# Letting the shared expert's products run until the first block's down products, and loading ScalarE's silu table ahead of that block

## The chip, the cores and the metric

One core of a Trainium2 chip runs one layer of a decoder in one launch. The metric is the device time of one execution in microseconds (us). The engines are named as in the profile: PE (TensorE matmul), PEld (its weight loads), DVE (VectorE), ACT (ScalarE), POOL (GpSimd), SP (SyncE, which issues the weight transfers).

## What is computed

The reference is one layer on 256 tokens of width 1024: a mixer (convolution, differential attention, gates), then a mixture of experts. The change touches the second half alone:

```python
def moe_ffn(h, ...):                       # t: 256 tokens x 1024
    scores = sigmoid(t @ w_router)         # 64 experts, group-limited top 8
    gates = ...                            # weight of each token for each expert, 0 for most
    g, u = split(t_e @ w_gu[e])            # each expert: 1024 -> 2 x 256
    routed += (silu(g) * u * gate) @ w_down[e]      # 256 -> 1024
    sg, su = split(t @ w_sh_gu)            # the shared expert, for all tokens
    shared = (silu(sg) * su) @ w_sh_down
    return routed + shared
```

Weights and activations are float32. The 64 experts' weights are 3 MB each (2 MB gate/up, 1 MB down), 192 MB in all, and each is read once.

## The kernel before

The kernel is written as some forty Python generators (fibers), one for each strand of work. A planner (class `Plan`, lines 49 to 184) runs them against its own costs and due times: each `yield` names an engine and a cost, an event or a buffer; whichever fiber can start first, or has the higher priority in `PRIO` among those that start nearly together, issues its instruction next. The order in which instructions are issued is the order in each engine's queue, which the engine then works through from the front. So a line that changes when an event is set can move instructions on every engine. On the chip, an instruction waits on semaphores for what it reads and for the buffer that it writes, not for the planner's events.

Once the router has chosen, the experts are grouped into 28 **blocks** of 128 token slots, by kind: P (two experts of 64 slots), H (one of 128), M, and Q (four of 32). Blocks 0, 1 and 2 are of kind P, block 3 of kind Q. `experts` (L1793 on) goes through the blocks in order, all on PE's queue. For a block it issues

- the gate/up products of all its experts (L1802, one pass over k = 0 to 7),
- the combine of the block before (L1710, which scatters the down products back to tokens), then the transposes of the block's activations (L1823), which wait for ACT's silu (L1672) and DVE's scaling (L1676),
- the gather of a later block's tokens (L1523) and that block's slot tables (L1564, L1567; a copy on ACT, L1584),
- the down products (L1849), which wait for ACT's copy of the transposes (L1685).

Weights are loaded by SP (L270) in one fixed list, in order, into 1 MB slots. A load waits in SP's queue until PE has read the last of what its slot held: after k = 3 or 7 of a gate/up pass, or after a block's down products, whose `done` frees their slots (here named late_w for blocks 0 and 2).

The **shared expert** is a fiber of priority 0, `shared` (L1771 on): 32 products of 128x256 (L1784; each stands as two rows in the trace), two halves of the weights by two halves of the tokens (bank 76 takes tokens 0 to 127, bank 79 the rest). When a half of the tokens is done, `shared_tail` (L1637 on, through `gate_up`) does silu on ACT, a product on DVE (L1619), two transposes (L1625), a copy on ACT (L1629) and four down products of 128x512 (L1647), each pair of which DVE scales (L1650) before POOL adds it (L1653). Before the change, `shared` goes on freely until block 0's tokens are gathered (event "blk" 0), and from then on waits for "static", which is set after block 3's gate/up.

`overflow` (L1443 on) lists the tokens for which an expert had no slot: a ladder of tiny products and DVE operations (L1446 to L1479). `gathers` (L1583 on) gathers the tokens of blocks 0 and 1 and then sets their "blk" events.

Of the kernel before, what the change touches and what calls it, by code (L numbers as in the profile page):

```python
# [13 lines left out]
AF = mybir.ActivationFunctionType  # L14
# [161 lines left out]
def TS(n):  # L176
    return "D", 0.13 + 0.00052 * n
# [10 lines left out]
def AP(n, table=None):  # L188
    return "A", 0.06 + 0.00082 * n, table
# [6 lines left out]
def MM(n):  # L196
    return "P", n / 2400.0
# [3 lines left out]
def tile_hybrid_block(ctx, tc, x, c, positions, w_ada, b_ada, norm1_g, w_in, conv_dw, conv_dw_b,  # L201
# [3 lines left out]
    nc = tc.nc  # L205
# [7 lines left out]
    pl = Plan()  # L213
# [246 lines left out]
    iop = cst.tile([P, 1], F32, name="iop")  # L460
# [826 lines left out]
    warm = cst.tile([P, 1], F32, name="warm")  # L1287
# [198 lines left out]
    def evacuate(xt, f, p, p3, ns, b0):  # L1486
        for f2 in range(2):
            k = f + f2
            e = yield TS(ns) if not b0 and f % 4 == 0 else AP(ns)
            if e == "A":  # L1490
                nc.scalar.activation(xt[:, k, 0:ns], p3[:, f2, 0:ns], AF.Identity, bias=b2c[:, k:k + 1],  # L1491
                                     scale=a2c[:, k:k + 1])
            else:
                nc.vector.tensor_scalar(xt[:, k, 0:ns], p3[:, f2, 0:ns], a2c[:, k:k + 1], b2c[:, k:k + 1],
                                        op0=OP.mult, op1=OP.add)
        pl.put("bank", p)
        pl.set("xt", b0, f // 2)
# [3 lines left out]
    def compare(b0, t, r_):  # L1501
        pm_ = tables[b0]
        for i, (kd, js) in enumerate(blocks[b0:b0 + 2]):
            rows = rows_of[kd]
            n, m = len(rows), rows[0][1]
            if kd == "M":
                yield "D", 0.4
                for j, (o, m) in zip(js, rows):
                    nc.vector.tensor_scalar(pm_[:, t, i * P + o:i * P + o + m], iot256[:, 0:m], r_[:, t, j:j + 1],
                                            None, op0=OP.is_equal)  # L1510
            else:
                yield TT(P)
                o = pm_[:, t, i * P:(i + 1) * P].rearrange("p (n m) -> p n m", n=n)
                nc.vector.tensor_tensor(o, iot256[:, None, 0:m].to_broadcast([P, n, m]),
                                        r_[:, t, js[0]:js[0] + n, None].to_broadcast([P, n, m]), op=OP.is_equal)

    def moved(b0, p, f, ts):
        ns = P * len(blocks[b0:b0 + 2])
        p3 = p.rearrange("p (f s) -> p f s", f=2)
        for f2 in range(2):  # L1520
            for t in ts:
                for a in range(2):
                    nc.tensor.matmul(p3[:, f2, 0:ns], xr[:, a, t, (f + f2) * P:(f + f2 + 1) * P],  # L1523
                                     tables[b0][:, t, 0:ns], start=(f2 + t + a == 0), stop=(f2 + t + a == 3))
        return p3

    def opened(b0, xt):
        users = [len(blocks[b0:b0 + 2])]
        for i in range(users[0]):
            info = Weights()  # L1530
            info.xt, info.whole, info.users = xt[:, :, i * P:(i + 1) * P], xt, users
            pl.events["info", b0 + i] = info
# [55 lines left out]
    def gathers():  # L1588
        tables[0] = yield Get("pm")
        held = []  # L1590
        for t in range(2):
            pl.cur.prio = PRIO["gathers" if t else "compare"]
            yield pl.ev("rx", t)
            yield from compare(0, t, rxp[0])
            for q in range(2):
                yield pl.ev("xr", t, q)
            if t:
                pl.set("first_pm")
                opened(0, (yield Get("xt")))
            for f in range(0, K, 2):  # L1600
                if not t:
                    held.append((yield Get("bank")))
                yield MM(4 * 2 * P)
                p3 = moved(0, held[f // 2], f, (t,))
                if t:
                    pl.spawn(evacuate(pl.events["info", 0].whole, f, held[f // 2], p3, 2 * P, 0))
        for b in range(2):
            pl.set("blk", b)
        for b in range(2):
            yield from slots(b)  # L1610
# [157 lines left out]
    def shared():  # L1768
        w = None
        pgs = []  # L1770
        for q in range(2):  # L1771
            for t in range(2):
                for k in range(4 * q, 4 * q + 4):
                    yield pl.ev("h2", t, k)
                    if not k:
                        pgs.append((yield Get("bank")))
                    yield pl.ev("L", "sg", 0, k // 2)
                    w = loaded["sg", 0]
                    yield w.at[k]
                    if pl.ev("blk", 0).t is not None:  # L1780
                        yield pl.ev("static")
                    for c_ in (slice(0, 256), slice(256, 512)):
                        yield MM(4 * 256)
                        nc.tensor.matmul(pgs[t][:, c_], h2T[:, k, t * P:(t + 1) * P], w.k[k][:, c_],  # L1784
                                         start=(k + c_.start == 0), stop=(k == K - 1 and c_.start > 0))
                if q:
                    pl.spawn(shared_tail(t, pgs[t]))
            done(("sg", 0), q)

    def experts():  # L1790
        for b, (kd, js) in enumerate(blocks):
            yield pl.ev("blk", b)
            info = pl.events["info", b]  # L1793
            pg = yield Get("bank")
            for k in range(K):
                yield pl.ev("xt", b - b % 2, k // 2)
                for j in js:
                    yield pl.ev("L", "g", j, k // 2)
                    yield loaded["g", j].at[k]
                yield "P", 0.87  # L1800
                for e, o, m in tiles_of[kd]:
                    nc.tensor.matmul(pg[o:o + m], info.xt[:, k, o:o + m], loaded["g", js[e]].k[k],  # L1802
                                     start=(k == 0), stop=(k == K - 1))
                if b < 2 and k % 4 == 1:
                    for j in js:
                        if loaded["g", j].off[k // 4] != LAST:
                            advance(pl.cur.ready, loaded["g", j].off[k // 4])
                if k % 4 == 3:
                    for j in js:
                        done(("g", j), k // 4)  # L1810
            if b == NS // 2:
                pl.set("static")
            info.users[0] -= 1
            if not info.users[0]:
                pl.put("xt", info.whole)
            pl.spawn(activate(b, pg))
            if b:
                for h in range(2):
                    yield from combine(b - 1, h)
            yield pl.ev("act", b)  # L1820
            yield "P", 0.3
            for f in range(2):
                nc.tensor.transpose(pg[:, f * P:(f + 1) * P], info.act.rearrange("s (c f) -> s f c", f=2)[:, f], ident)  # L1823
            pl.put("act", info.act)
            pl.spawn(turned(b, pg))
            ahead = b + 2 - b % 2
            if ahead < len(blocks):
                if ahead == 2:
                    fs = (0, 2, 4, 6) if b else ()
                else:  # L1830
                    fs = (4, 6) if b % 2 else (0, 2)
                if fs:
                    yield from moves(ahead, fs)
            if 2 <= b + 1 < len(blocks):
                yield from slots(b + 1)
            yield pl.ev("aT", b)
            if b == len(blocks) - 1:
                yield pl.ev("slots", b)
                yield from finale(js, info, info.aT)
                return  # L1840
            pd = yield Get("bank", 2)
            for j in js:
                yield pl.ev("L", "d", j, 0)
                yield max(loaded["d", j].at)
            for f in range(2):
                for h in range(2):
                    yield "P", 0.87
                    for e, o, m in tiles_of[kd]:
                        nc.tensor.matmul(pd[h][o:o + m], info.aT[:, f, o:o + m],  # L1849
                                         loaded["d", js[e]].k[f][:, h * 512:(h + 1) * 512],  # L1850
                                         start=(f == 0), stop=(f == 1))
            for j in js:
                done(("d", j), 0)
            pl.put("aT", info.aT)
            pl.spawn(scaled(b, pd))
# [145 lines left out]
```

## Time and profile before

| | |
|---|---|
| median of 3 runs (lowest to highest) | 820.47 us (818.65 to 822.19) |
| the profiled execution | 819.49 us, span 817.7 us, granted PE clock 0.969 on the mean |
| PE busy | 766.1 us (94% of the span), 4759 matmuls |
| DVE, ACT, POOL busy | 444.6 us, 324.9 us, 192.4 us |
| moved by DMA | 271.04 MB, 331 GB/s over the span; 420 to 422 GB/s in most slices from 410 us on |
| mixer and router | 0 to about 337 us |
| blocks 0 to 27 and the output | about 337 to 817.7 us |

A matmul's end is modelled, so PE counts as busy while matmuls follow each other. "PEclk" is the granted clock, 1.00 for 2.4 GHz and 0.50 for 1.2 GHz. "DMA" is the mean busy share of 16 DMA engines. A row's time in brackets, with an arrow, is the idle time of its engine before it and what ended it. The page's chain that ended last has no rows in this profile.

### The profile page before, as it was taken

How to read it: one execution, taken by the hardware profiler on the slowest of the kernel's cores; microseconds unless marked ns; L12 is line 12 of the kernel's file. 1: busy time of each engine (PE TensorE's matmuls, PEld its weight loads, DVE VectorE, ACT ScalarE, POOL GpSimd, SP SyncE). 2: the span in 40 equal slices, each digit the busy share in tenths (PEclk: the TensorE clock that was granted, in tenths of full speed). 3: DMA queues.
4: the chain of work that ended last, by engine and by line, in shares of the span. 5: the costliest groups of instructions: out<-in, count | busy, mean ns of one | idle time of the engine just before them, and what ended most of it. 6: DMA issues, size and time to landing. Idle time of an engine off the chain costs nothing.

```text
span 817.7 us, 13180 instructions
## 1 busy us (share of the span) xinstructions
PE 766.1 (94%) x4759; PEld 469.8 (57%) x4759; DVE 444.6 (54%) x1035; ACT 324.9 (40%) x713; POOL 192.4 (24%) x246
## 2 busy tenths in 40 slices
PE   3999999899996999999999797999999999999997
PEld 2898777589784987545454141354464455444543
DVE  5458998999996677433433141344344344433443
ACT  4356656865759755223221021232232232232220
POOL 3003788888572693000002000000000000000000
PEclk9999999899997999989999898999999999999999
DMA  9998776546654676469999999999999999999993
GB/s 312 365 336 288 261 253 227 180 161 227 228 184 155 239 280 252 165 245 390 390 420 420 422 421 420 421 422 420 420 421 422 421 420 421 420 421 419 419 413 139
DMA packets 69883, 271.04 MB, mean 331 GB/s; under 512 B 6085, under 2 KB 15893, under 8 KB 46520
## 3 DMA queue, kind: packets, MB, share of 16 engines
q1 hardware_dynamic: 69464, 270.00, 84.9%
q8 instruction: 38, 0.62, 0.3%
q0 software_dynamic: 304, 0.16, 0.1%
q14 instruction: 29, 0.24, 0.1%
q10 hardware_dynamic: 48, 0.01, 0.0%
HBM read 269.11 MB, written 1.05 MB: 330 GB/s over the span
## 4 chain that ended last, share of the span: by engine, by line


## 5 line engine op out<-in xcount | busy, mean ns | idle before, releaser
L1802 PE MATMUL bank<-fa 128*32 128x512 f32 (+2 forms) x1048 | 203.7, 608 | 8.3 <-DMA fa<-in_w_exp_gu_dram 8.3
L1802 PEld LDWEIGHTS bank<-fa 128*32 128x32 f32 (+2 forms) x1048 | 60.3, 124 | 132.1 <-issue 107.3
L863 DVE SCALAR_TENSOR_TENSOR bank<-fa,tap,bank 128x256 f32<-128x256 f32 x232 | 112.9, 486 | 6.1
L1676 DVE SCALAR_TENSOR_TENSOR fa<-bank,gsc,h 128x256 f32<-128x256 f32 x28 | 13.5, 484 | 170.1 <-ACT h L1672 170.1
L1849 PE MATMUL bank<-fa 128*32 128x512 f32 (+1 forms) x496 | 83.9, 596 | 0.0
L1672 ACT ACTIVATE h<-bank 128x256 f32<-128x256 f32 x28 | 10.8, 385 | 179.7 <-PE bank L1802 179.7
L776 POOL TENSOR_TENSOR rb<-fa,rb 128x512 fp32r<-128x512 f32 x46 | 60.2, 1317 | 65.6 <-ACT rb L795 64.6
L1694 DVE TENSOR_TENSOR fa<-bank,fa 128x512 f32<-128x512 f32 x54 | 37.4, 692 | 65.5 <-PE bank L1849 62.7
L776 POOL TENSOR_TENSOR ra<-fa,ra 128x512 fp32r<-128x512 f32 x48 | 63.9, 1339 | 20.5 <-ACT ra L795 17.1
L1762 ACT CAST obs<-fa 128x512 fp32r<-128x512 f32 x54 | 33.4, 618 | 83.7 <-DVE fa L1694 83.7
L1719 DVE TENSOR_TENSOR fa<-fa,bank 128x512 f32<-128x512 f32 x108 | 66.7, 678 | 0.0
L1491 ACT ACTIVATE fa<-bank,b2c,a2c 128x256 f32<-128x256 f32 x108 | 53.6, 561 | 20.8 <-PE bank L1523 20.8
L795 ACT CAST ra<-fa 128x512 fp32r<-128x512 f32 x76 | 46.8, 622 | 37.0 <-PE bank L812 22.9
L1523 PE MATMUL bank<-ra 128*128 128x256 f32 x448 | 60.5, 288 | 0.0
L1710 PE MATMUL bank<-obs,ra 128*128 128x512 f32 x216 | 58.3, 412 | 0.0
L795 ACT CAST rb<-fa 128x512 fp32r<-128x512 f32 x68 | 42.0, 623 | 37.8 <-PE bank L812 22.4
L1802 PE MATMUL bank<-late_w,fa 128*32 128x512 f32 (+2 forms) x168 | 51.9, 627 | 4.1 <-DMA late_w<-in_w_exp_gu_dram 4.1
L1523 PEld LDWEIGHTS bank<-ra 128*128 128x128 f32 x448 | 55.6, 191 | 0.2
L1710 PEld LDWEIGHTS bank<-obs,ra 128*128 128x128 f32 x216 | 38.7, 188 | 28.8 <-issue 21.5
L811 PE MATMUL bank<-ra 128*128 128x256 f32 x160 | 47.8, 299 | 1.9 <-ACT ra L577 1.8
L1849 PEld LDWEIGHTS bank<-fa 128*32 128x32 f32 (+1 forms) x496 | 22.8, 119 | 41.1 <-issue 35.3
L811 PE MATMUL bank<-ra,rb 128*128 128x256 f32 x160 | 46.1, 288 | 0.0
(376 smaller groups left out, 1391.5 us busy)
## 6 DMA issues: line engine op xcount, KB each, us to landing
fa<-in_w_exp_gu_dram SPq DMA_DIRECT2D x100, 1024.0 KB, 19.8
fa<-in_w_exp_down_dram SPq DMA_DIRECT2D x50, 1024.0 KB, 19.8
fa<-in_w_ada_dram SPq DMA_DIRECT2D x24, 1024.0 KB, 7.9
fa<-in_w_in_dram SPq DMA_DIRECT2D x22, 1024.0 KB, 5.3
late_w<-in_w_exp_gu_dram SPq DMA_DIRECT2D x17, 1024.0 KB, 19.3
late_w<-in_w_exp_down_dram SPq DMA_DIRECT2D x12, 1024.0 KB, 6.8
fa<-in_w_exp_gu_dram SPq DMA_DIRECT2D x22, 512.0 KB, 9.4
fa<-in_w_in_dram SPq DMA_DIRECT2D x12, 512.0 KB, 9.4
```

The costliest lines, as they stand in the source:

```text
L776: (nc.gpsimd if e == "G" else nc.vector).tensor_tensor(hl[:, 1], w.k[k], hl[:, 0].bitcast(F32), op=OP.subtract)
L795: nc.scalar.copy(hl[:, 0], w.k[k])
L811: nc.tensor.matmul(o, hl[:, 0, mm], src_t[:, k, 0], start=(k == 0 and m % 2 == 0), stop=False)
L863: nc.vector.scalar_tensor_tensor(cv[:, m] if j == TAPS - 1 else acc, u_sb[:, m, j:j + T], tap[:, m, j:j + 1], acc, op0=OP.mult, op1=OP.add)
L1491: nc.scalar.activation(xt[:, k, 0:ns], p3[:, f2, 0:ns], AF.Identity, bias=b2c[:, k:k + 1], scale=a2c[:, k:k + 1])
L1523: nc.tensor.matmul(p3[:, f2, 0:ns], xr[:, a, t, (f + f2) * P:(f + f2 + 1) * P], tables[b0][:, t, 0:ns], start=(f2 + t + a == 0), stop=(f2 ...
L1694: nc.vector.tensor_tensor(o32, pd[h], g2b[:, h * 512:(h + 1) * 512], op=OP.mult)
L1710: nc.tensor.matmul(p, info.pT[:, t * P:(t + 1) * P], ob[a], start=(a == 0), stop=(a == 1))
L1719: nc.vector.tensor_tensor(x_sb[:, t, d], x_sb[:, t, d], p, op=OP.add)
L1762: nc.scalar.copy(ob[0], o32)
L1802: nc.tensor.matmul(pg[o:o + m], info.xt[:, k, o:o + m], loaded["g", js[e]].k[k], start=(k == 0), stop=(k == K - 1))
L1849: nc.tensor.matmul(pd[h][o:o + m], info.aT[:, f, o:o + m], loaded["d", js[e]].k[f][:, h * 512:(h + 1) * 512], start=(f == 0), stop=(f == 1))
```

## The change

```diff
@@ gathers @@
                 if t:
                     pl.spawn(evacuate(pl.events["info", 0].whole, f, held[f // 2], p3, 2 * P, 0))
+        yield AP(1, "silu")
+        nc.scalar.activation(warm, iop, AF.Silu)
         for b in range(2):
             pl.set("blk", b)
@@ shared @@
                     w = loaded["sg", 0]
                     yield w.at[k]
-                    if pl.ev("blk", 0).t is not None:
+                    if pl.ev("down", 0).t is not None:
                         yield pl.ev("static")
@@ experts @@
                                          start=(f == 0), stop=(f == 1))
+            pl.set("down", b)
             for j in js:
                 done(("d", j), 0)
```

ACT gets a silu of one column, whose result nobody reads, with the table load in front of it, ahead of the events that start block 0. `shared` now goes on until block 0's down products have been issued, and waits for "static" from then on. Line numbers behind the first edit are two higher in the changed file, behind the last one three (L1784 is L1786 there, L1849 is L1851).

The planner then orders the queues anew. On PE three places change up to block 3; the rest of the queue keeps its order of blocks.

**PE ahead of block 0's gate/up.** First the queue before, then the changed one. L1784 (L1786) are the shared expert's products, L1416 and L1421 turn the gates for the slot tables, L1802 (L1804) is block 0's gate/up:

```order
L1784 MATMUL bank_76<-fa 128x256
L1416 MATMUL bank_78<-ident,fa 64x128 x2
L1802 MATMUL bank_75<-fa 64x512 x2
L1421 MATMUL bank_77<-fa 128x64 x2
L1802 MATMUL bank_75<-fa 64x512 x7
```

```order
L1786 MATMUL bank_76<-fa 128x256
L1416 MATMUL bank_78<-ident,fa 64x128 x2
L1786 MATMUL bank_76<-fa 128x256 x2
L1421 MATMUL bank_77<-fa 128x64 x2
L1786 MATMUL bank_76<-fa 128x256 x2
L1804 MATMUL bank_75<-fa 64x512 x9
```

Four products of the shared expert now stand ahead of block 0's gate/up; they are the last of the first 128 tokens.

**PE between block 0's gate/up and its down products.** L1564 and L1567 are the slot tables of blocks 0 and 1, L1446 to L1462 the overflow's ladder, L1823 (L1825) the transposes, L1849 (L1851) the down products. Before, then changed:

```order
L1564 MATMUL bank_74<-ra 128x4 x2
L1567 MATMUL bank_74<-ident,ra 128x128 x2
L1446 MATMUL bank_73<-fa 64x1
L1447 MATMUL bank_73<-iop,fa 64x1
L1455 LDWEIGHTS trib
L1455 MATMUL bank_73<-ovb,trib 64x1
L1461 MATMUL bank_73<-fa 1x64
L1462 MATMUL bank_73<-ones,fa 1x1
L1823 MATMUL bank_75<-ident,fa 128x128 x2
L1849 MATMUL bank_78<-late_w,fa 64x512 x2
```

```order
L1564 MATMUL bank_74<-ra 128x4 x2
L1567 MATMUL bank_74<-ident,ra 128x128 x2
L1786 MATMUL bank_79<-fa 128x256
L1825 MATMUL bank_75<-ident,fa 128x128 x2
L1786 MATMUL bank_79<-fa 128x256
L1851 MATMUL bank_78<-late_w,fa 64x512 x2
```

The ladder is gone from here; one product stands ahead of the transposes and one behind them.

**PE between block 2's gate/up and its down products.** L1823 (L1825) are block 2's transposes; L1627 and L1649 in the changed file are L1625 and L1647 of the file before, the shared expert's transposes and down products; L1474 and L1479 end the overflow's ladder, L1523 gathers tokens of block 4. Before, then changed:

```order
L1823 MATMUL bank_80<-ident,fa 128x128 x2
L1474 MATMUL bank_73<-ident,fa 64x128 x2
L1479 MATMUL bank_73<-fa 128x64 x2
L1523 MATMUL bank_78<-ra 128x256 x8
L1523 MATMUL bank_77<-ra 128x256 x8
```

```order
L1825 MATMUL bank_80<-ident,fa 128x128 x2
L1786 MATMUL bank_79<-fa 128x256 x2
L1627 MATMUL bank_76<-ident,fa 128x128 x2
L1446 MATMUL bank_73<-fa 64x1
L1447 MATMUL bank_73<-iop,fa 64x1
L1649 MATMUL bank_78<-fa 128x512 x2
L1455 LDWEIGHTS trib
L1455 MATMUL bank_73<-ovb,trib 64x1
L1461 MATMUL bank_73<-fa 1x64
L1462 MATMUL bank_73<-ones,fa 1x1
L1649 MATMUL bank_77<-fa 128x512 x2
L1474 MATMUL bank_73<-ident,fa 64x128 x2
```

Two more products, the tail of the first 128 tokens and the whole ladder now stand ahead of block 2's down products. Behind them four products are left of the 32 (12 before), inside block 4's gate/up and behind its down products, and the tail of the other tokens, inside block 5's gate/up (where both tails stood before).

On DVE, the scaling of the first pair of shared down products (L1650; L1652 in the changed file) stands between L1453 and L1457 of the ladder. On ACT, the table load, the silu of one column and the shared expert's silu stand between L1418 and block 0's silu, and block 0's silu stands ahead of the two copies L1584, which stood ahead of it. On SP the reading of the overflow's count (L1947) leaves its place ahead of block 2's first load for the end of the loads; the loads themselves stand in the same order up to block 4.

## Rows read from the trace of the kernel before

**Rows 1.** The windows view: busy time and instructions of each engine in three stretches (us of the span), then the granted PE clock (1.00 is 2.4 GHz), the DMA share and GB/s.

```profile
350.00:355.00 5.00, 4.94 (x14) 1.54 (x16) 0.23 (x1) 0.01 (x1) 0.00 (x0) 0.54 0.03 10
...
388.00:392.00 4.00, 4.00 (x32) 1.09 (x32) 2.67 (x4) 1.24 (x2) 0.00 (x0) 1.00 0.70 242
...
400.00:530.00 130.00, 116.61 (x651) 49.55 (x651) 37.76 (x82) 25.92 (x56) 5.09 (x4) 0.95 1.01 421
```

**Rows 2.** What PE waited for from 392 to 530 us (its first two rows), and from 530 us to the end (the one row that there is): us in total, times, longest.

```profile
PE bank L1802 <- DMA fa<-in_w_exp_gu_dram: 8.3, 8, 1.5
PE bank L1802 <- DMA late_w<-in_w_exp_gu_dram: 4.1, 3, 1.4
...
PE bank L1735 <- ACT fa L1685: 0.5, 1, 0.5
```

**Rows 3.** The timeline of PE: the last row that waited for weights (start us, us, engine, line, operation, count, idle before).

```profile
527.64 0.64 PE L1802 MATMUL bank<-late_w,fa 128*64 128x512 f32 x1 [1.30 <-DMA late_w<-in_w_exp_gu_dram]
```

**Rows 4.** The timeline from block 0's slot tables to block 1's gate/up (columns as above).

```profile
344.74 0.38 PE L1564 MATMUL bank<-ra 128*128 128x4 f32 x2
...
345.53 0.16 DVE L1577 SCALAR_TENSOR_TENSOR gsc<-bank,bmaskP 128x4 f32<-128x4 f32 x1 [5.96 <-PE bank L1567]
...
345.74 0.79 ACT L1584 CAST ra<-bank 128x256 fp32r<-128x256 f32 x2 [8.02 <-DVE gsc L1577]
...
345.77 0.27 PE L1446 MATMUL bank<-fa 64*64 64x1 f32 x2
...
346.53 1.28 ACT L1672 ACT_TABLE_LOAD   x1
...
347.82 0.38 ACT L1672 ACTIVATE h<-bank 128x256 f32<-128x256 f32 x1
348.32 0.48 DVE L1676 SCALAR_TENSOR_TENSOR fa<-bank,gsc,h 128x256 f32<-128x256 f32 x1 [0.72 <-ACT h L1672]
...
348.86 0.70 PE L1823 MATMUL bank<-ident,fa 128*128 128x128 f32 x2 [0.89 <-DVE fa L1676]
...
349.64 0.37 ACT L1685 COPY fa<-bank 128x256 f32<-128x256 f32 x1 [1.43 <-PE bank L1823]
...
350.06 5.89 PE L1849 MATMUL bank<-late_w,fa 128*64 128x512 f32 x16 [0.51 <-ACT fa L1685]
...
355.79 2.74 PE L1802 MATMUL bank<-fa 128*64 128x512 f32 x12
...
355.99 0.81 SPq L270 DMA_DIRECT2D late_w<-in_w_exp_down_dram  x2
```

**Rows 5.** The windows view again, one microsecond each, ahead of and behind the fall of the granted clock.

```profile
346.00:347.00 1.00, 0.19 (x4) 0.10 (x3) 1.00 (x9) 0.95 (x3) 0.00 (x0) 1.00 1.02 418
...
348.00:349.00 1.00, 0.14 (x1) 0.14 (x2) 0.68 (x3) 0.21 (x1) 0.00 (x0) 0.50 1.02 418
```

**Rows 6.** The timeline at the start of block 0's gate/up.

```profile
336.99 1.08 PE L1802 MATMUL bank<-fa 128*64 128x512 f32 x4
...
338.00 0.66 PE L1421 MATMUL bank<-fa 64*128 64x64 f32 x4
...
338.58 3.22 PE L1802 MATMUL bank<-fa 128*64 128x512 f32 x13
```

**Rows 7.** The timeline, prices of what is moved: the shared expert's products and parts of the overflow's ladder.

```profile
318.43 3.67 PE L1784 MATMUL bank<-fa 128*128 128x256 f32 x16
...
347.17 0.15 DVE L1457 COPY fa<-bank 64x1 f32<-64x1 f32 x1
...
347.66 0.28 PE L1461 MATMUL bank<-fa 64*1 64x64 f32 x2 [0.53 <-DVE fa L1459]
...
348.72 0.20 DVE L1464 CAST olist<-bank 1x65 int32<-1x65 f32 x1
...
350.01 0.23 DVE L1471 TENSOR_TENSOR fa<-fa 128x64 f32<-128x64 f32 x1
```

**Rows 8.** The timeline of the shared expert's tail as it stands before, inside block 5's gate/up: transposes (L1625), down products (L1647), scaling (L1650).

```profile
430.27 1.98 PE L1647 MATMUL bank<-fa 128*128 128x512 f32 x4 [0.51 <-ACT fa L1629]
...
432.09 0.39 PE L1625 MATMUL bank<-ident,fa 128*128 128x128 f32 x2
...
432.30 0.69 DVE L1650 TENSOR_TENSOR fa<-bank,fa 128x512 f32<-128x512 f32 x1 [1.88 <-PE bank L1647]
...
432.94 1.98 PE L1647 MATMUL bank<-fa 128*128 128x512 f32 x4 [0.46 <-ACT fa L1629]
```

**Rows 9.** The timeline around block 2's down products, and SP's loads from block 0's down products to block 2's.

```profile
357.70 19.63 SPq L270 DMA_DIRECT2D fa<-in_w_exp_gu_dram  x12
...
379.85 1.16 SPq L270 DMA_DIRECT2D fa<-in_w_exp_down_dram  x2
...
381.74 0.39 PE L1823 MATMUL bank<-ident,fa 128*128 128x128 f32 x2
...
383.44 2.18 PE L1523 MATMUL bank<-ra 128*128 128x256 f32 x16
...
385.97 3.65 PE L1849 MATMUL bank<-late_w,fa 128*64 128x512 f32 x16
...
389.55 7.07 PE L1802 MATMUL bank<-fa 128*32 128x512 f32 x64
...
389.65 0.90 SPq L270 DMA_DIRECT2D late_w<-in_w_exp_down_dram  x2
```

## The prediction, before the run

> **What bounds the kernel now.** The page's chain has no rows, so I read the bound stage by stage: first the windows view, then PE's waits, then the timeline of the two places that the change touches. From 400 us on the DMA engines are busy all the time (share 1.01, 421 GB/s), while PE, over the same 130 us, stands for some 13 us [rows 1]. What it stands for are gate/up weights: 8.3 + 4.1 = 12.4 us in eleven waits, the last of them, 1.30 us, ending at 527.64; from 530 us to the end PE waits for no weights at all, 0.5 us for ACT apart [rows 2, 3]. So up to 527.6 us the time is set by the stream of weights, behind that by PE's own queue, which can start no earlier than that last load lands. When that load lands is fixed by the stream's last interruption ahead of it. One is plain: at 350 to 355 us the DMA share is 0.03, because SP waits for block 0's down products (they start at 350.06, block 1 follows at 355.79, and SP issues at 355.99) [rows 1, 4]. The last one, a short one, is at 388 to 392 us with a share of 0.70: SP has issued everything that it had slots for and waits for block 2's down products, which make way for block 3 at 389.55; SP issues at 389.65 [rows 1, 9]. From there the stream is never interrupted again. **Whatever the change does ahead of block 2, the end moves with the moment at which block 2's down products are over.** That is the sum to make.
>
> **Term 1, four products ahead of block 0.** One product is two rows of the trace, 3.67 / 16 = 0.229 us a row [rows 7]: 8 rows make 1.83 us. Of that 0.13 us fills a wait: four gate/up rows from 336.99 and one of 0.22 us each (28 rows from 338.58 to 344.74) end at 337.87, and L1421 starts at 338.00 [rows 4, 6]. Cost: **1.70 us**, so block 0's slot tables start at 346.44 instead of 344.74. The table load of 1.28 us with the silu of one column goes into ACT's idle 8.02 us ahead of L1584 [rows 4], which also takes the shared expert's silu. Were that cover gone, block 0's silu would wait for it as it does now.
>
> The Trainium skill (ScalarE: Activation LUTs, What ACT_TABLE_LOAD costs) gives a switch of tables 2.66 us, a load of 1.28 and a drain of 1.38. The trace has the load with 1.28 and the silu at once behind it, at 347.82 [rows 4], no drain. If the moved switch cost 2.66, the change would save 1.4 us more and the result would be 822.8.
>
> **Term 2, from the slot tables to the down products.** Before, 350.06 - 344.74 = 5.32 us: ACT's two copies, table load, silu, scaling, transposes and copy stand one behind the other [rows 4]. After, block 0's silu is ahead of the copies and needs no load. The first slot table gives DVE its gate at 345.53 + 1.70 = 347.23, 0.17 us later the scaling starts (0.48 us), so transposes at about 347.93. PE meanwhile has slot tables up to 345.77 + 1.70 = 347.47 and one product of 0.46 us: no wait to speak of. ACT's second copy L1584 needs the second gate, which DVE makes behind the scaling (to about 348.1): 0.40 us, then the copy of the transposes, 0.37 us: 348.9. The down products start at about 348.95, behind the second product. Gain against 350.06: **1.11 us**, term 1 being taken off already.
>
> **Term 3, the clock in block 0's down products.** They take 355.79 - 350.06 = 5.73 us at a granted clock of 0.54, that is mostly at 1.2 GHz; block 2's equal ones take 389.55 - 385.97 = 3.58 us at 1.00 [rows 1, 4, 9]. The clock fell after PE had been busy 0.19 of a microsecond, and stood at 0.50 while it was busy 0.14 [rows 5]. After the change PE's longest wait there is the 0.3 us ahead of the down products (product done at 348.65), so I take 3.58; the other end is 5.73, no gain. Gain: **2.15 us**. Block 1 starts 1.11 + 2.15 = **3.3 us** earlier, and so does the first load behind it. SP's reading of the overflow's count leaves the place ahead of that load, but SP stood there for block 0's products anyway: nothing.
>
> **Term 4, what now stands ahead of block 2's down products.** Between block 2's transposes and the gather L1523 there were 1.70 us (381.74 to 383.44), the ladder's last two steps [rows 9]; these stay. New are, each in PE's queue:
> - two products, four rows: 0.92 [rows 7];
> - the shared transposes up to the down products that wait for their copy on ACT, 432.09 to 432.94: 0.85; the ladder's first step lies in it [rows 8];
> - one pair of shared down products, 430.27 to 432.09: 1.82 [rows 8];
> - the ladder's middle. DVE scales that pair ahead of it: the pair's last row ends 0.16 us later, scaling 0.69, then 0.49 from L1457 to L1461 (347.17 to 347.66) [rows 7, 8]: with the handing over about 1.35;
> - L1461 and L1462: 0.22;
> - the second pair: 1.82. Behind it L1474 would wait for DVE's 1.52 us (348.72 to 350.24) [rows 7]; the 1.82 hide it.
>
> Together **7.0 us**. Lower end 5.7: should DVE run the ladder ahead of the scaling, the 1.35 shrink towards nothing. Upper end 10.2: with the clock at half (second rival). I take 7.0, because every piece has a row at the full clock.
>
> Could the stream run on meanwhile? Between block 0's and block 2's down products SP has slots for 2, 12 and 2 loads; of the 12, eight are halves of 0.5 MB (every load of block 3's first half), so 12 MB in all, 12.6 million bytes [rows 4, 9]. At 421 GB/s [rows 1] they take 30 us. Restarted at about 354 us, they are through by 385, and block 2's down products end near 393: the stream stands for about 8 us there. So the delay is fully paid.
>
> **Sum.** Block 2's down products end 7.0 - 3.3 = 3.7 us later, and with them the stream, the load that PE awaits at 527.64, and the end. Less work of the shared expert behind block 2 gives nothing back: it comes off a stretch in which PE waits 12.4 us. The profiled execution's own 819.49 us becomes 823.2. That execution lies 0.98 us under the median of 820.47; for the median the forecast is **824.2 us**, 0.45% more. A measurement of this kernel can tell about 0.5%, 4.1 us, from no change, so this stands just inside it.
>
> **Rivals.**
> *PE sets the pace (faster).* If the stream no longer made PE wait, the work taken from behind block 2 would count: eight products (3.67 us) and one tail (0.85 + 2 x 1.82 = 4.49), 8.2 us. 3.7 - 8.2 = -4.5: 816.0. It decides if PE's waits for weights behind block 2 add up to less than 8.2 us; rows 2 have 12.4, and a stream that restarts 3.7 us later adds to them. For it speaks that PE is unbroken from 530 us on. Chance 0.10.
> *The clock falls in block 2's section (slower).* PE waits there for ACT's copy (0.46 us in the row at 432.94) and about 1.2 us for DVE in the ladder, both between gate/up and down products, as at block 0. If the granted clock falls on that and comes back as late as at block 0, where the down products alone lost 2.15 us and the transposes ahead of them ran at half clock too, the section takes 2.2 to 3.5 us more: at 3.2, 827.4. It decides from the point at which these waits leave PE as idle as in the microseconds of the fall. Those have it 0.14 to 0.19 busy [rows 5], while here 1.8 us of products stand on either side of the longer wait, which speaks against it. Chance 0.13.
> The Trainium skill (TensorE: Matmul & The Clock Gate, A second HAM failure mode: psum-queue depth-cycling) says that frequent short idles between groups of matmuls are enough to make the clock go back and forth. By that rule block 2's section is in danger.
> *The short interruption at 388 us is not what the stream hangs on.* Then only terms 1 to 3 count: 820.47 - 3.3 = 817.2. Against it stands SP's issue 0.1 us after block 3's start, with the share at 0.70 [rows 1, 9]. Chance 0.07.
>
> **How the numbers follow.** Forecast 0.70, the rivals 0.10, 0.13, 0.07. Around 824.2 the terms are uncertain by about 1 us and the medians by more than one (818.65 to 822.19), so of the 0.70 some 0.28 lies above 824.6, with 0.11 of the clock's: slower 0.39. Faster than 816.4: half of the first rival and a little of the third, 0.08. The rest, 0.53, is no change that can be told. The range, 819.5 to 828.0, holds the forecast with term 4's lower end and the scatter, and the clock; it leaves out the faster rivals.
>
> **What would show it.** Right: no table load between block 0's gate/up and its silu; down products of block 0 in about 3.6 us at clock 1.00, block 1 at about 352.5; block 2's down products over near 393; a DMA share far under 0.70 in the 8 us ahead of that, and 1.01 after it; PE's last wait for weights still near 530 us. Wrong: waits for weights gone behind 400 us (first rival), a PEclk of 0.5 between 378 and 393 (second), or a DMA stream that goes through block 2's section (third).

## The result, and the profile after

| | changed kernel | kernel before | ratio, 95% interval |
|---|---|---|---|
| first comparison, median | 825.70 us (7 times, 823.72 to 828.44) | 820.47 us (7) | 1.0060 (1.0041 to 1.0079) |
| second comparison, `r_after` | 827.91 us (6 times, 825.58 to 829.77) | 820.31 us (23) | 1.0096 (1.0072 to 1.0120) |
| profiled execution, span | 823.9 us, clock 0.972 | 817.7 us, clock 0.969 | |

The change makes the kernel slower: the medians are 5.2 and 7.6 us apart. The forecast was 824.2 us with a range of 819.5 to 828.0: both medians lie in it, above its middle, the second one by only 0.1 us under its upper end.

**The stream.** The windows view of the changed kernel, columns as in [rows 1]:

```profile
350.00:355.00 5.00, 4.92 (x26) 1.66 (x26) 1.77 (x6) 1.04 (x3) 0.00 (x0) 1.00 0.61 248
384.00:388.00 4.00, 1.95 (x10) 1.08 (x10) 3.33 (x10) 0.00 (x0) 1.26 (x1) 1.00 0.96 406
388.00:392.00 4.00, 3.55 (x27) 2.92 (x25) 1.08 (x3) 1.41 (x4) 1.28 (x1) 1.00 0.03 12
392.00:396.00 4.00, 4.00 (x22) 1.26 (x25) 1.73 (x8) 1.35 (x4) 0.00 (x0) 1.00 0.00 0
400.00:530.00 130.00, 113.22 (x650) 47.10 (x644) 38.72 (x83) 26.11 (x56) 2.52 (x2) 0.95 1.01 421
```

The DMA share at 350 to 355 us rises from 0.03 to 0.61 and the clock from 0.54 to 1.00: block 0's end is better. At 388 to 392 the share falls from 0.70 to 0.03, and nothing is moved until 396: there the stream stands. From 400 us on it is as before, 1.01 and 421 GB/s. PE's waits from 392 to 535 us (sum, times, longest), and then the last of them on PE's timeline:

```profile
PE bank L1804 <- DMA fa<-in_w_exp_gu_dram: 11.4, 11, 1.6
PE bank L1804 <- DMA late_w<-in_w_exp_gu_dram: 4.3, 3, 1.4
PE bank L1851 <- DMA fa<-in_w_exp_down_dram: 1.4, 2, 0.7
```

```profile
534.03 2.37 PE L1804 MATMUL bank<-fa 128*64 128x512 f32 x10 [1.32 <-DMA fa<-in_w_exp_gu_dram]
```

The waits have grown from 12.4 to 17.1 us, since eight products and one tail are gone from here: from block 3's start to the last of these waits PE is busy 120.1 us instead of 124.7. (The prediction counts 8.2 us for what is gone; PE's busy time fell by 4.6.) That last wait ends at 534.03 instead of 527.64 [rows 2, 3]: 6.4 us later, as the span is 6.2 us longer. From block 3's start it is 138.2 us to there, 138.1 before: less work did not bring it nearer.

**Block 0's end** (timeline: start, duration; answers to [rows 4]):

```profile
348.08 0.38 PE L1564 MATMUL bank<-ra 128*128 128x4 f32 x2
348.22 0.38 ACT L1674 ACTIVATE h<-bank 128x256 f32<-128x256 f32 x1 [6.67 <-PE bank L1804]
349.62 0.51 PE L1825 MATMUL bank<-ident,fa 128*128 128x128 f32 x2
350.22 0.37 ACT L1687 COPY fa<-bank 128x256 f32<-128x256 f32 x1 [0.17 <-PE bank L1825]
350.64 3.65 PE L1851 MATMUL bank<-late_w,fa 128*64 128x512 f32 x16
354.13 0.60 PE L1804 MATMUL bank<-fa 128*64 128x512 f32 x2
354.32 0.33 SPq L270 DMA_DIRECT2D late_w<-in_w_exp_down_dram  x1
```

From slot tables to down products it takes 2.56 us instead of 5.32, and the down products 3.49 instead of 5.73. **Block 2's section** (answers to [rows 9]):

```profile
380.08 0.39 PE L1825 MATMUL bank<-ident,fa 128*128 128x128 f32 x2
380.31 1.03 PE L1786 MATMUL bank<-fa 128*128 128x256 f32 x4
381.18 0.39 PE L1627 MATMUL bank<-ident,fa 128*128 128x128 f32 x2
382.08 1.98 PE L1649 MATMUL bank<-fa 128*128 128x512 f32 x4 [0.20 <-ACT fa L1631]
384.00 0.19 PE L1455 MATMUL bank<-ovb,trib 64*64 64x1 bf16 x1
384.88 1.26 POOL L1655 TENSOR_TENSOR fa<-fa 128x512 f32<-128x512 f32 x1 [56.89 <-DVE fa L1457]
384.89 1.29 DVE L1459 TENSOR_SCALAR fa<-iot,fa 64x64 f32<-64x64 f32 x1
386.24 0.27 PE L1461 MATMUL bank<-fa 64*1 64x64 f32 x2 [2.05 <-DVE fa L1459]
386.46 1.98 PE L1649 MATMUL bank<-fa 128*128 128x512 f32 x4
388.29 0.38 PE L1474 MATMUL bank<-ident,fa 128*64 128x128 f32 x2
389.71 2.17 PE L1523 MATMUL bank<-ra 128*128 128x256 f32 x16
392.22 3.65 PE L1851 MATMUL bank<-late_w,fa 128*64 128x512 f32 x16
395.80 0.64 PE L1804 MATMUL bank<-fa 128*32 128x512 f32 x4
395.90 0.33 SPq L270 DMA_DIRECT2D late_w<-in_w_exp_down_dram  x1
```

From the transposes to the gather L1523 it is now 9.63 us, where it was 1.70. SP issues again at 395.90, 0.10 us after block 3's start, as before.

### The profile page after: what moved, and what is told of

The parts are those of the page before. It is cut to its first block, busy times and chain, and to the rows that moved or that the text cites. A ratio compares the mean times of both kernels' runs of the same rounds, so it can differ in the third digit from the quotient of the medians.

```text
span 823.9 us, 13173 instructions
## 1 busy us (share of the span) xinstructions
PE 767.9 (93%) x4759; PEld 470.9 (57%) x4759; DVE 449.3 (55%) x1035; ACT 325.0 (39%) x714; POOL 192.6 (23%) x246
## 3 DMA queue, kind: packets, MB, share of 16 engines
HBM read 269.11 MB, written 1.05 MB: 328 GB/s over the span
## 4 chain that ended last, share of the span: by engine, by line
## 5 line engine op out<-in xcount | busy, mean ns | idle before, releaser
L1804 PE MATMUL bank<-fa 128*32 128x512 f32 (+2 forms) x1040 | 200.1, 612 | 11.4 <-DMA fa<-in_w_exp_gu_dram 11.4
L1804 PEld LDWEIGHTS bank<-fa 128*32 128x32 f32 (+2 forms) x1040 | 59.3, 126 | 136.3 <-issue 106.1
L1851 PE MATMUL bank<-fa 128*32 128x512 f32 (+2 forms) x504 | 82.2, 597 | 1.4 <-DMA fa<-in_w_exp_down_dram 1.4
L1523 PE MATMUL bank<-ra 128*128 128x256 f32 x448 | 60.5, 288 | 0.0
L1523 PEld LDWEIGHTS bank<-ra 128*128 128x128 f32 x448 | 55.5, 191 | 0.2
L811 PE MATMUL bank<-ra 128*128 128x256 f32 x160 | 48.4, 302 | 1.9 <-ACT ra L577 1.8
L1851 PEld LDWEIGHTS bank<-fa 128*32 128x32 f32 (+2 forms) x504 | 22.5, 119 | 44.9 <-issue 36.5
L812 PE MATMUL bank<-ra 128*128 128x256 f32 x160 | 46.4, 290 | 0.1
L813 PE MATMUL bank<-ra 128*128 128x256 f32 x160 | 46.2, 289 | 0.0
```

The source lines that it names most:

```text
L811: nc.tensor.matmul(o, hl[:, 0, mm], src_t[:, k, 0], start=(k == 0 and m % 2 == 0), stop=False)
L812: nc.tensor.matmul(o, hl[:, 0, mm], src_t[:, k, 1], start=False, stop=False)
L813: nc.tensor.matmul(o, hl[:, 1, mm], src_t[:, k, 0], start=False, stop=last)
L1851: nc.tensor.matmul(pd[h][o:o + m], info.aT[:, f, o:o + m], loaded["d", js[e]].k[f][:, h * 512:(h + 1) * 512], start=(f == 0), stop=(f == 1))
```

## The experiments

Theory: the end hangs on the moment at which block 2's down products are over. First rival: PE's work in all sets the pace. The table holds all profiled executions, in us, worked out from starts on PE: "front" is L1416 to block 0's slot tables, "gap" from there to its down products, "down 0" these until block 1 starts, "section" from block 2's transposes to its down products, "sum" L1416 to block 3's start (with 25.95 from block 1 to the transposes and 3.6 of block 2's down products, alike in all but e1_table_only, where these take 3.9). In the two kernels with the ladder at a higher priority its first step, 0.3 us, counts to the front. "Rest" is the span less block 3's start.

| kernel | L1416 at | front | gap | down 0 | section | sum | block 3 at | span | rest |
|---|---|---|---|---|---|---|---|---|---|
| before | 336.68 | 8.06 | 5.32 | 5.73 | 4.23 | 52.87 | 389.55 | 817.7 | 428.15 |
| r_before | 338.64 | 8.06 | 5.33 | 5.48 | 4.23 | 52.64 | 391.28 | 819.4 | 428.12 |
| changed | 338.24 | 9.84 | 2.56 | 3.49 | 12.14 | 57.56 | 395.80 | 823.9 | 428.10 |
| r_after | 337.66 | 9.84 | 2.57 | 3.48 | 13.80 | 59.24 | 396.90 | 824.8 | 427.90 |
| e6_no_add | 338.34 | 9.84 | 2.57 | 3.49 | 11.11 | 56.55 | 394.89 | 823.1 | 428.21 |
| r_no_add | 339.02 | 9.84 | 2.57 | 3.48 | 11.10 | 56.54 | 395.56 | 823.7 | 428.14 |
| e1_table_only | 335.34 | 8.91 | 2.66 | 3.48 | 10.05 | 54.95 | 390.29 | 818.4 | 428.11 |
| e2_products_only | 338.87 | 8.07 | 5.11 | 3.49 | 12.68 | 58.88 | 397.75 | 825.7 | 427.95 |
| e3_tail_late | 340.23 | 9.83 | 2.67 | 3.48 | 10.15 | 55.67 | 395.90 | 824.4 | 428.50 |
| e4_tail_late_ladder | 340.23 | 10.16 | 2.67 | 3.48 | 4.51 | 50.36 | 390.59 | 818.9 | 428.31 |
| e5_dummy2 | 337.68 | 8.07 | 5.23 | 4.73 | 7.68 | 55.25 | 392.93 | 820.9 | 427.97 |
| e5_dummy5 | 336.70 | 8.06 | 5.33 | 5.77 | 4.23 | 52.92 | 389.62 | 817.7 | 428.08 |
| e7_table_ladder | 340.07 | 8.38 | 2.67 | 3.48 | 4.23 | 48.29 | 388.36 | 816.8 | 428.44 |

**The rest is 427.9 to 428.5 us in all thirteen**, whether 2 products or 20, and one tail or two, stand behind block 2. The start of L1416 scatters from 335.3 to 340.2, and by 2.0 us between two executions of the same kernel before; it goes with the granted clock ahead of it: over the first 330 us this was 0.964 on the mean where L1416 came first (e1_table_only), 0.959 and 0.953 in the two executions of before, 0.954 in both of the changed kernel and 0.943 in e4_tail_late_ladder, one of the two where it came last. The second execution of before starts L1416 later (338.64) than either execution of the changed kernel, so the first profiles' difference of 1.56 us is not put down to the change.

### Twice the same products, at two places

```diff
@@ experts, before the down products @@
+            if b == 2:                       # e5_dummy5: b == 5
+                pq = yield Get("bank")
+                for _ in range(8):
+                    yield MM(4 * 256)
+                    nc.tensor.matmul(pq[:, 0:256], h2T[:, 0, 0:P], g2b[:, 0:256], ...)
+                pl.put("bank", pq)
             yield pl.ev("aT", b)
```

> The kernel before with eight idle products more, of the shared products' shape (128x256, 3.67 us together by the rows of those), ahead of block 2's down products; their result is not used. Theory (the end hangs on the end of block 2's down products): block 3 starts 3.7 us later and the end comes 3.7 us later, ratio 1.0045; the span less the start of block 3 stays at the 428.1 us of the kernel before. Rival (PE's total work sets the pace): also 3.7 us more, told apart only by the run with the same products further on.

> The kernel before with the same eight idle products ahead of block 5's down products, near 445 us, behind the last interruption of the stream and ahead of PE's last wait for weights. Theory: PE's waits for weights behind them shrink by 3.7 us in sum, the stream and the end stay where they were, within 0.5 us: ratio 1.000 to 1.001. Rival (PE's total work sets the pace): 3.7 us more, ratio 1.0045.

Measured: 824.53 us, ratio 1.0041 (1.0024 to 1.0058) ahead of block 2's down products; 820.79 us, ratio 1.0003 (0.9987 to 1.0019) ahead of block 5's. The same 3.62 us of products cost 3.5 us at the one place and nothing at the other: PE's work in all is not the pace, block 2's end is. (In the table the section of e5_dummy2 is 3.45 us longer, the sum only 2.38, because block 0's down products happened to take 4.73 us in that execution.) One detail came out otherwise: PE's waits for weights in 392 to 530 us sank by 0.5 us only (12.4 to 11.9). PE's busy time over 400 to 530 us rose by as little, from 116.6 to 117.2, at a mean clock of 0.97 instead of 0.95; that the higher clock took the products up is read from these two numbers, not tested. The products at the two places:

```profile
385.80 3.62 PE L1840 MATMUL bank<-fa 128*128 128x256 f32 x16
443.02 3.62 PE L1840 MATMUL bank<-fa 128*128 128x256 f32 x16
```

### The two halves of the change

```diff
@@ e1_table_only: gathers; the gate of shared as before @@
+        pl.table = "silu"
+        nc.scalar.activation(warm, iop, AF.Silu)
```

> The kernel before plus the silu of one column ahead of the first block, nothing else: PE's order is that of before, all eight products, the tail and the ladder stay where they were. Theory (the stream hangs on the end of block 2's down products): the table load of 1.28 us leaves block 0's chain, so block 1 starts 1.3 us earlier, 3.4 us if the granted clock no longer falls over block 0's down products (then these take 3.6 instead of 5.7 us); nothing is added to block 2's section. End 1.3 to 3.4 us under the kernel before, ratio 0.996 to 0.9985. Rival (PE sets the pace behind block 2, so moving the stream changes nothing): the same time as before. Rival on the offset seen ahead of block 0 (it comes with the added ScalarE operation): block 0's gate/up start 1 to 1.6 us later than before, and the kernel gains nothing.

Measured: 823.75 us, ratio 1.0028 (1.0007 to 1.0048): slower, where a gain was expected. Block 0 gained, 15.05 us from L1416 to block 1 (8.91 + 2.66 + 3.48) instead of 19.11, and by more than the 1.3 to 3.4 expected. But the expectation described the kernel wrongly: with the table taken as loaded (`pl.table` is the planner's note of it) the planner put the ladder's middle into block 2's section. Its timeline:

```profile
378.19 0.27 PE L1461 MATMUL bank<-fa 64*1 64x64 f32 x2 [1.34 <-DVE fa L1459]
379.44 0.30 PE L1474 MATMUL bank<-ident,fa 128*64 128x128 f32 x1 [0.96 <-DVE fa L1471]
380.87 1.11 PE L1479 MATMUL bank<-fa 64*128 64x64 f32 x4 [0.46 <-ACT fa L1476]
381.91 3.78 PE L1523 MATMUL bank<-ra 128*128 128x256 f32 x16
```

PE waits 3.1 us in four places, and the gather takes 3.78 us instead of 2.17, at half clock. The section costs 5.8 us more, block 0's part gives 4.1, although the table load, here ahead of L1418, makes L1421 wait 0.77 us. So the ladder leaves the gap even without the products. L1416 starts at 335.34, earlier than in any other execution: the rival on the offset is refuted.

```diff
@@ e2_products_only, against the changed kernel: the gate of shared stays, gathers as before @@
-        yield AP(1, "silu")
-        nc.scalar.activation(warm, iop, AF.Silu)
```

> The change without the silu of one column: the shared products and the tail move, the table load of 1.28 us stays in block 0's chain. The order that comes of it has no product ahead of block 0's gate/up, one more in block 0's gap, and tail and ladder in block 2's section as in the changed kernel. Theory: block 2's section is about 8 us longer than before (9.6 instead of 1.7 from its transposes to the gather), of which some of the ladder's place in block 0's gap comes back (about 2 us); end about 5 to 6 us over the kernel before, ratio 1.006 to 1.008. Rival (PE sets the pace): 4 to 5 us under the kernel before, since eight products and one tail are gone from behind block 2.

Measured: 828.39 us, ratio 1.0086 (1.0057 to 1.0114). The sum is 6.0 us over before, the section 12.68: the sum as expected, the ratio a little above the 1.006 to 1.008. Where the products went was not: eight of them stand in block 0's gap, where the changed kernel has two and one more was expected. The gap keeps its table load and takes 5.11 us, so the sum is 58.88 where the first profile of the changed kernel has 57.56. By the medians the two kernels can't be told apart (1.0086 against 1.0060 and 1.0096).

### Where the tail and the ladder stand

Both edits are made to the changed kernel.

```diff
@@ e3_tail_late: shared_tail @@
+        yield pl.ev("static")
         aT = yield from gate_up(pg, None)
@@ e4_tail_late_ladder: in addition @@
-        "overflow": 0,
+        "overflow": 5,
```

> The changed kernel with the shared expert's tail held back until block 3 has begun, as it was before; the two products and the whole ladder stay in block 2's section. Theory: the section loses 0.85 + 1.82 + 1.82 us of PE's work of the tail, and the operation of VectorE that stood beside GpSimd's addition (1.29 us) goes back to some 0.25 us, since no addition runs there: 5 to 5.5 us shorter than in the changed kernel. End 820.5 to 821, ratio to the kernel before 1.000 to 1.001. Rival (PE sets the pace, the total of its work counts): no better than the changed kernel, ratio 1.006, since the same work is only moved behind.

> As the kernel with the late tail, and the overflow's ladder goes back into block 0's gap (its priority raised), so that only two products and the ladder's last two steps stand in block 2's section. Theory: block 1 starts about 3 us earlier than in the kernel before (no table load, full clock over block 0's down products, less 1.7 us of products ahead of block 0), block 2's section is 0.9 us longer: end 2 to 2.5 us under the kernel before, some 818, ratio 0.997 to 0.998. Rival (PE sets the pace): ratio 1.00 or more.

Measured: 824.88 us, ratio 1.0043 (1.0024 to 1.0062), and 818.87 us, ratio 0.9969 (0.9951 to 0.9988). With the ladder in block 0's gap it came as expected. Without the tail alone it did not: the section lost 2.0 us, not 5 to 5.5. The expectation forgot that the tail's products also cover the ladder's waits. Bare, they are 0.61 + 0.52 + 0.96 + 0.35 + 0.46 = 2.9 us, and behind them the clock falls, to 0.50 at 389 to 391 us, and the gather takes 3.64 us instead of 2.17 (timeline of e3_tail_late):

```profile
384.36 0.16 PE L1455 MATMUL bank<-ovb,trib 64*64 64x1 bf16 x1 [0.61 <-DVE ovb L1453]
386.30 0.30 PE L1474 MATMUL bank<-ident,fa 128*64 128x128 f32 x1 [0.96 <-DVE fa L1471]
388.29 3.64 PE L1523 MATMUL bank<-ra 128*128 128x256 f32 x16
```

### The long DVE operation

The changed kernel without POOL's additions of the first tail; their share is left out of the output.

```diff
@@ e6_no_add, r_no_add: shared_tail @@
+            if shared_left[0] == 1:
                 (nc.gpsimd if e == "G" else nc.vector).tensor_tensor(x_sb[:, t, d], x_sb[:, t, d], tm, op=OP.add)
```

> The changed kernel without GpSimd's two additions of the first tail (the shared expert's share of one half of the tokens is left out of the output); the order on PE, VectorE and ScalarE is that of the changed kernel. Theory (VectorE's L1459 takes 1.29 us because GpSimd's 128x512 addition runs beside it): L1459 takes about 0.25 us as in the kernel before, L1461 comes 1.0 us sooner behind L1455, block 2's section is 1.0 us shorter: from L1416 to block 3's start 56.5 us instead of 57.6, the end some 1 us under the changed kernel, ratio to the kernel before 1.004 to 1.005. Rival (L1459 is long for a reason of its own in that place, such as reading what PE has just written): it stays at 1.29 us and nothing moves.

Measured: 826.66 us (4 times), ratio 1.0069 (1.0051 to 1.0087), no less than the changed kernel; its profile, however, has the section 1.03 us shorter. The same kernels again, in the same rounds:

> The kernel before once more, for a second profiled execution. Theory: from the start of L1416 (block 0's columns) to block 3's start it needs about 52.9 us again, less where the clock falls for a shorter time over block 0's down products (between 3.6 and 5.9 us); the span less block 3's start is 428.1 us; the start of L1416 itself scatters with the clock granted ahead of it (335 to 340 us in the executions so far). Rival (the start of L1416 belongs to the kernel): 336.7 us again.

> The changed kernel once more, beside the kernel before in the same rounds. Theory: 57.5 us from L1416 to block 3's start, 4.7 us more than before, the clock at 1.00 through both sections; end 4.5 to 5 us over the kernel before, ratio 1.0055 to 1.006. Rival (the 1.56 us by which L1416 started later in its first profile belong to the change): 338.2 us for L1416 again, and a ratio that the 4.7 us do not explain.

> The changed kernel without GpSimd's two additions of the first tail once more (their share is left out of the output), beside the changed kernel in the same rounds, since four times of the first look gave 826.66 us against a section that is 1.0 us shorter. Theory: 56.5 us from L1416 to block 3's start, 1.0 us under the changed kernel, and so the end, ratio to the kernel before about 1.0045. Rival (what the ladder wins is lost again in a place that the section does not show): the median of the changed kernel or more.

Measured: 820.50 us, ratio 1.0003 (0.9985 to 1.0021); 827.91 us, ratio 1.0096; 824.11 us (12 times), ratio 1.0039 (1.0022 to 1.0057). L1416 starts at 338.64 in r_before and not at 336.7 again, which refutes that run's rival. The kernel without the additions came to 826.66 in one comparison and to 824.11 in the other: medians of a few runs do not settle 1 us, the sections do. The timeline of r_no_add:

```profile
385.50 0.14 DVE L1457 COPY fa<-bank 64x1 f32<-64x1 f32 x1
385.67 0.25 DVE L1459 TENSOR_SCALAR fa<-iot,fa 64x64 f32<-64x64 f32 x1
385.97 0.27 PE L1461 MATMUL bank<-fa 64*1 64x64 f32 x2 [1.00 <-DVE fa L1459]
386.20 1.98 PE L1649 MATMUL bank<-fa 128*128 128x512 f32 x4
```

Without POOL's addition L1459 takes 0.25 us instead of 1.29, and PE waits 1.00 instead of 2.05. The same place in r_after:

```profile
384.31 1.26 POOL L1655 TENSOR_TENSOR fa<-fa 128x512 f32<-128x512 f32 x1 [56.90 <-DVE fa L1457]
384.32 1.30 DVE L1459 TENSOR_SCALAR fa<-iot,fa 64x64 f32<-64x64 f32 x1
385.67 0.27 PE L1461 MATMUL bank<-fa 64*1 64x64 f32 x2 [2.06 <-DVE fa L1459]
385.90 3.63 PE L1649 MATMUL bank<-fa 128*128 128x512 f32 x4
```

and r_after's windows view (PE's busy time is the second figure, the clock the third from the end):

```profile
384.00:385.00 1.00, 0.00 (x0) 0.00 (x0) 0.96 (x3) 0.00 (x0) 0.69 (x1) 1.00 0.97 410
385.00:386.00 1.00, 0.33 (x5) 0.30 (x5) 0.61 (x1) 0.00 (x0) 0.57 (x1) 0.91 0.99 418
386.00:387.00 1.00, 1.00 (x2) 0.48 (x3) 0.93 (x5) 0.00 (x0) 0.00 (x0) 0.50 1.08 451
```

The hold is the same, but here the clock falls to 0.50 behind it, and the second pair takes 3.63 us instead of 1.98; the section is 1.66 us longer. The hold thus costs 1.0 us each time, and in this execution the clock on top. That the hold brings the clock down is not shown: of three profiles with a wait of 2.05 us or 2.06 here (the two of the changed kernel, e2_products_only) the clock fell in one, and in e1_table_only and e3_tail_late it fell without the hold. The expectation for r_after (clock 1.00, 57.5 us) did not hold. The medians of the same rounds stand 3.8 us apart; the two profiles explain 2.7 of it, the rest is open within the scatter.

### The part that pays, alone

```diff
@@ e7_table_ladder: behind the copy L1418 @@
         nc.scalar.copy(gatT, p[0:NE, 0:T])
+        pl.table = "silu"
+        nc.scalar.activation(warm, iop, AF.Silu)
@@ PRIO @@
-        "overflow": 0,
+        "overflow": 5,
```

> The kernel before with the silu of one column behind ScalarE's copy L1418, ahead of block 0's gate/up, and the overflow's ladder held in block 0's gap by a higher priority; no product of the shared expert is moved, the tail stays behind block 3. Theory: block 0's part as in the run with the table alone (6.1 to 6.5 us from slot tables to block 1, instead of 11.05), block 2's section as in the kernel before (1.7 us from transposes to gather): from L1416 to block 3's start 48.2 to 48.5 us instead of 52.87. End 4.4 to 4.7 us under the kernel before, 816.4 to 816.7, ratio 0.9945. Rival (the clock falls again, in block 0's gap or in block 2's section, since PE stands there for VectorE and ScalarE): up to 2 us less gain, ratio 0.997. Rival (PE sets the pace): no gain, ratio 1.000.

Measured: 817.91 us, ratio 0.9953 (0.9935 to 0.9970), faster than the kernel before in the same rounds, and under both medians of the changed one. The sum is 48.29, as worked out, 4.58 us less than before; the medians are 3.1 us apart and the ratio stands for 3.9, so the end came a little later than the 816.4 to 816.7 expected, and that part is not explained by the sections. The timeline shows two short waits left in the gap and none of the ladder's middle in the section:

```profile
350.10 0.51 PE L1825 MATMUL bank<-ident,fa 128*128 128x128 f32 x2 [0.43 <-DVE fa L1459]
351.12 3.65 PE L1851 MATMUL bank<-late_w,fa 128*64 128x512 f32 x16 [0.22 <-ACT fa L1687]
```

## Why the prediction was right, and where it was off

**The bound** held: the rest of 428 us is the same in thirteen executions, and equal products cost all or nothing by their place. So the mechanism was right, and a size in its sum was off.

**Term 1** (1.70): 9.84 - 8.06 = 1.78. **Term 2** (1.11 gained, net of term 1): L1416 to block 0's down products 13.38 before, 12.40 after: 0.98. **Term 3** (2.15): 5.73 - 3.49 = 2.24 against the first profile; the four executions with before's block 0 have 4.73 to 5.77, so the clock's fall there differs from execution to execution and the gain is 1.2 to 2.3; that 2.15 came out so closely is owed to taking forecast and check from the same execution. Together block 1 came 3.22 us sooner, 3.3 forecast. The table load lay under ACT's idle time with no drain behind it: 1.28 us from 339.29, the silu of one column at 340.58. The 2.66 us of the Trainium skill (ScalarE: Activation LUTs, What ACT_TABLE_LOAD costs) are not in this trace either.

**Term 4** (7.0) was mis-sized: 7.93 us more between transposes and gather. Piece by piece, forecast and measured: products 0.92 and 0.87; transposes to the first pair 0.85 and 0.90; first pair 1.82 and 1.92; **the ladder's middle 1.35 and 2.24**; L1461 and L1462 0.22 and 0.22; second pair 1.82 and 1.83. The step that failed is the one that took "0.49 from L1457 to L1461" from block 0's gap [rows 7], where POOL was idle. In the new place the first pair's scaling, whose result POOL's addition L1655 reads, is done at the very moment at which DVE comes to L1459 (POOL's row names L1457, which ended last on DVE). Without the addition the middle is 385.31 - 384.12 = 1.19 us in e6_no_add, so the scaling itself was rightly counted and the hold is the 1.05 us between 1.19 and 2.24. The Trainium skill has a rule for it that the prediction left out (SBUF — State Buffer, Who interferes with whom): DVE in some of its modes and GpSimd share a pair of ports, and whichever issues first holds it for its whole instruction while the other "fully blocks". The trace agrees: POOL from 384.88 to 386.14, L1459 to 386.18. In which mode L1459 runs, no run here shows.

**Sum**: 3.7 forecast, 57.56 - 52.87 = 4.69 in the first profiles. Against the first comparison's medians (825.70 - 820.47 = 5.23, interval 3.4 to 6.5) that is enough. The profiles' own difference, 6.2 us, holds 1.56 more from the scatter of L1416. In the second profiles the sum is 59.24 - 52.64 = 6.60, against medians 7.60 apart (interval 5.9 to 9.8). That the second median still lies in the range is owed to the room left upward for the clock, not to the size of term 4.

**Rivals.** *PE sets the pace*: refuted by the pair of dummy runs and by the growth of PE's waits from 12.4 to 17.1 us. *The interruption at 388 us is not decisive*: refuted by the constant rest. *The clock falls in block 2's section*: not in the first profile, but in the second, with 1.66 us, below the 2.2 to 3.5 given to it. The prediction priced it as a property of the kernel; it comes in some executions and not in others. Of seven profiles with the ladder's middle in that section it fell in three (r_after, e1_table_only, e3_tail_late). The second comparison's 827.91 stands beside the 827.4 of this rival, but whether the clock fell there in more than the one execution profiled is not shown: that one, at 826.62, was among the faster of the six. By the rule of the Trainium skill on frequent short idles (TensorE: Matmul & The Clock Gate, A second HAM failure mode: psum-queue depth-cycling) the section was in danger: the traces agree in those three and not in the other four. What tells the executions apart stays open: PE was busy 0.18, 0.00 and 0.76 of the microseconds from 384 in the first profile, clock 1.00, and 0.00 and 0.33 in r_after before the fall.

**The two halves**: the early table load gains and the moved products lose, but the load too loses (1.0028) where the planner may then put the ladder into block 2's section. Held in the gap, it gives 0.9953.

## What to carry to other kernels

When a prefetching stream is the bound, find the last point at which it has run out of free buffers, and count only what stands ahead of the release there. Here 3.6 us of PE's work cost 3.5 us in front of that point and nothing 55 us behind it. A list of waiting steps that is free in a gap becomes the bound when the gap is closed: say where each step goes, and what its neighbours on other engines do at that moment, before a duration is carried from the old place to the new one. In a kernel ordered by a planner an edit of one line moves others; look at the order that comes of it, not at the edit.

## What the runs showed of the hardware

A DVE operation on 64x64 elements in SBUF took 0.25 us alone and 1.29 to 1.30 us when POOL's 128x512 addition had started 0.01 us ahead of it; both ended within 0.05 us of each other. Around the same wait of PE, 2.05 and 2.06 us, the granted clock stayed at 1.00 throughout in one execution and stood at 0.50 for some three microseconds in another (386 to 389 us in r_after). And the start of L1416, ahead of which none of the edits stands in PE's queue, lay anywhere from 335.3 to 340.2 us: single profiles of this kernel can't be compared by their spans, but by the length of a section they can, to 0.1 us where the clock is the same.
